# A hybrid decoder layer on one core: eight small edits of order in a kernel that keeps TensorE full

## The chip, the core and the metric

The kernel runs on one of the cores of a Trainium2 chip. Four engines compute: TensorE (PE in the profile, its weight loads PEld), VectorE (DVE), ScalarE (ACT) and GpSimd (POOL). SyncE (SP) only issues transfers. Each engine works through a queue of its own in order and waits on semaphores for the others. [...]

The metric is the time of one launch on the device in microseconds, the median of several runs. A profiled execution of the same program gives the trace, and its span runs from the first instruction to the last.

## What is computed

One decoder layer (`DEPTH` is 1) is applied to 512 prompt tokens and to 64 sample tokens (8 sequences of 8), 576 in all, with shared weights and a width of 1024. Cut to what matters:

```
u    = rms(x) * g_pre_mix
proj = u @ w_in                      # z, conv channels, dt, q, k, v, gates, og
y    = mamba2_ssd(conv(xbc), dt, state)          * silu(z), normed
h    = mlstm(q, k, v, igate, fgate, state), normed * sigmoid(og)
x    = x + rms(concat(y, h) @ w_out) * g_post_mix
x    = x + rms(cross_attention(rms(x)*g, memory) @ w_xo) * g_post_x
u    = rms(x) * g_pre_ffn
x    = x + rms((silu(u @ w_gate) * (u @ w_up)) @ w_down) * g_post_ffn
```

Everything is float32, and besides `y` the states, the convolution tails and the memory keys and values are returned.

## The kernel before

**Number format.** A float32 product is made of three: each operand is split into a high part (the rounded format that TensorE takes at full rate) and a low part, the rest. The kernel computes high·high, high·low and low·high. A weight tile of 128 x 1024 comes by DMA into a `raw` buffer (two of them, a ring), ScalarE casts the high part into a `whi` buffer (three) and VectorE, or a DMA that accumulates, makes the low part in a `wlo` buffer (three). `split_w` (lines 178 to 194) is this chain, and `gemm` (line 201) is the products: per weight block two with the high part, then one with the low part. With its argument `late` it puts the low products of the first blocks behind all of their high ones.

**Stages.** The input projection (tiles of `win`) with convolution and gates runs to about 97 us of the trace. The Mamba heads follow (`ssd_prompt`, lines 624 to 693, with the sample states beside them, lines 712 to 805), to about 252 us, while TensorE also gets the q, k, v tiles as filling work. The mLSTM heads, the z and og gates and the output projection come next, then memory keys, attention and its projection `xo` (to about 700 us), and the feed-forward part to the end. In that last part gate, up and down products are done with a scheme of seven products in place of eight (`class Seven`, from line 1803): a pair of tiles is cut into blocks, sums of blocks are split into high and low parts, and `mul` (lines 1878 to 1887) does one of the seven products, number `w` of 0 to 6. `Down` uses blocks of three weight columns (`nk` is 3); `early` does products 0, 1, 3 and 2, `late` 5 and 6, `mid` 4.

**What sets the order.** Outside of blocks under `manual_schedule` a planner orders each engine's queue: it walks through a plan in which every instruction has a cost and a priority by its place in the program, and gives an engine what is ready there. `tc.issue_after(ins)` adds an edge to this: what the block traces *on the engine of* `ins` is queued behind it. It is an order in that engine's queue, no wait for completion, and instructions on other engines get no edge. Waits on data, and on a buffer's former readers, are added by the framework. Under `manual_schedule` (from the second half of `xo` to the first pairs of the feed-forward part, and at the very end) the order is written by hand through positions given to `at_`. The planner works on the whole program, so an edit early on can move the order further down.

**Places that the edits touch.** The start (lines 303 to 341) issues products of zeros into `ps_warm`, and loads `par` (gains and small constants), two weight tiles in four pieces each and the eight pieces of `xraw`. In the gate rows (lines 524 to 582) `cumst` and `sxst` hold a row sum in three bfloat16 pieces; `sx` also goes into `r1`, whose transposes become `CT`. In `ssd_prompt` each head gets a mask `lm` of 128 x 512: four sums on VectorE (L670), an exponential on ScalarE (L672), and a product with `cbs` on VectorE (L673), kept in the list `mults`; TensorE multiplies with it in `ps_yi` (L678). Beside it GpSimd scales the sample states:

```
with tc.issue_after(mults[7].ins) if b == 2 else ExitStack():
    G.tensor_tensor(hn, hn, decs[:, :, bb:bb + 1].to_broadcast([P, 16, 64]), op=ALU.mult)
```

`z_evac` (L1050) takes a z tile out of PSUM, and its first step is a VectorE product with `rxb` (L1053). `wm_split` (L1271) loads and splits four weight tiles for the memory keys and values. `xo` (L1528) makes the projection after attention; tiles 0, 1 and 2 hold the three PSUM buffers of the pool `g`, and each is taken out by a ScalarE square (L270 or L274) and a ScalarE copy (L1540).

Of the kernel before, what the change touches and what calls it, by code (L numbers as in the profile page):

```python
# [11 lines left out]
F32 = mybir.dt.float32  # L12
F32R = mybir.dt.float32r
BF16 = mybir.dt.bfloat16
AF = mybir.ActivationFunctionType
ALU = mybir.AluOpType
# [3 lines left out]
P = 128  # L20
# [4 lines left out]
KT = 8  # L25
# [81 lines left out]

CUT = 512
CCUT = 128
NWARM = 21  # L110
NSS = 7
NWX = 3
TCOPT = dict(schedule_with_timeline_sim=True)
# [2 lines left out]
def build(nc, tc, ctx, I, O):  # L116
    V, A, G, S, TE = nc.vector, nc.scalar, nc.gpsimd, nc.sync, nc.tensor
    mm = TE.matmul
# [12 lines left out]
    def SL(slot, name, dt=F32, shape=(P, KT, T)):  # L131

        return big.tile(list(shape), dt, name=name, tag="s%d" % slot, bufs=1)
# [29 lines left out]
    def PAR(k, j=None, w=1):  # L163
        a, b = _cols[k]
        return par[:, a:b] if j is None else par[:, a + j:a + j + w]
# [12 lines left out]
    def split_w(src, n=1024, cut=CUT, acc=False, pool=None, to=None, raw=None):  # L178
        if raw is None:
            raw = wp.tile([P, 1024], F32, name="raw", tag="raw", bufs=2)  # L180
        loads.append(S.dma_start(raw[:, :n], src))
        if to:
            split(*to, raw[:, :n])
            return to
        hi, lo = hi_lo(pool)
        casts.append(A.copy(hi[:, :n], raw[:, :n]))  # L186
        for e, a, b in ((V, 0, cut), (G, cut, n)):
            if b > a and e is G and acc:

                A.activation(lo[:, a:b], hi[:, a:b].bitcast(F32), AF.Copy, scale=-1.0)  # L190
                accs.append(G.dma_start(lo[:, a:b], src[:, a:b], accum_op=ALU.add))  # L191
            elif b > a:
                e.tensor_tensor(lo[:, a:b], raw[:, a:b], hi[:, a:b].bitcast(F32), op=ALU.subtract)  # L193
        return hi, lo
# [112 lines left out]
    psw = MP("ps_warm")  # L307
    for _ in range(NWARM):
        mm(psw[:, 0:256], wz[:, 0:128], wz, start=True, stop=True, skip_group_check=True)
    S.dma_start(par, I["par"])  # L310

    wl = [wp.tile([P, 1024], F32R, name="wlo", tag="wlo", bufs=3) for _ in range(2)]
    RT = {k: wp.tile([P, 3], F32, name=k + "_r", tag=k + "_r") for k in ("px0", "p30", "px1", "p31")}
# [2 lines left out]
    for k in range(KT):  # L316
        if k % 2 == 0:
            c = slice(128 * k, 128 * k + 256)
            S.dma_start(raws[0][:, c], I["win"][1][:, c])
        xd = (S if k else A).dma_start(xraw[:, k, :], I["xT"][:, k, :])  # L320
        if k % 2 == 0:
            xd = (S if k else A).dma_start(raws[1][:, c], I["win"][2][:, c])
        if k == 0:
            with tc.issue_after(xd.ins), tc.high_priority(offset=300):

                A.activation(sp.tile([P, 1], F32, name="one"), wz[:, 0:1], AF.Exp)

        if k == 0:
            V.tensor_copy(wi[0][0][:, c], raws[0][:, c])
        for t0, n in ([(0, T)] if k else HALVES):  # L330
            ts_ = slice(t0, t0 + n)
            uhk = A.activation(uh[:, k, ts_], xraw[:, k, ts_], AF.Copy, scale=PAR("g_pre", k))
            ulk = V.scalar_tensor_tensor(ul[:, k, ts_], xraw[:, k, ts_], PAR("g_pre", k), uh[:, k, ts_].bitcast(F32),
                                         op0=ALU.mult, op1=ALU.subtract)
        if k % 2 == 0:
            for i in range(2):
                with tc.issue_after(uhk.ins), tc.issue_after(ulk.ins):
                    split(wi[i][0][:, c], wi[i][1][:, c], raws[i][:, c], cast=None if k or i else lambda *_: None)
# [219 lines left out]
    V.tensor_copy(mp[r4, 512:576].rearrange("p (c t) -> p c t", t=8), m0.unsqueeze(2).to_broadcast([4, 8, 8]))  # L558
    sx = row("sx", tag="la")
    V.tensor_tensor(sx[r4, :], cum[r4, :], mrw[r4, :], op=ALU.subtract)  # L560
    V.tensor_tensor(sx[r4, :], sx[r4, :], mp[r4, :], op=ALU.add)
    V.tensor_tensor(gpr[r4, :], ig[r4, :], cum[r4, :], op=ALU.subtract)
    V.tensor_tensor(gpr[r4, :], gpr[r4, :], mp[r4, :], op=ALU.subtract)
    r2 = row("r2", 4, tag="i2")
# [7 lines left out]
    for st_, src, n in ((cumst, cum[0:16, :], 16), (sxst, sx[r4, :], 4)):  # L572
        b0 = 32 if n == 4 else 0
        bt, d1 = btt[b0:b0 + n, :], d1t[b0:b0 + n, :]
        G.memset(st_, 0.0)
        V.tensor_copy(bt, src)
        A.copy(st_[0:n, :], bt)
        V.tensor_tensor(d1, src, bt, op=ALU.subtract)
        V.tensor_copy(bt, d1)
        A.copy(st_[32:32 + n, :], bt)  # L580
        V.tensor_tensor(d1, d1, bt, op=ALU.subtract)
        A.copy(st_[64:64 + n, :], d1)
# [41 lines left out]
    def ssd_prompt(g):  # L624
# [35 lines left out]
        for j in range(4):  # L660
            jj = g * 4 + j
            psi = MP("ps_yi")
            lms = []
            for k in range(2):
                h = 2 * jj + k
                psb = MP("ps_l")
                mm(psb, sel[:80, h:h + 1].to_broadcast([80, P]), cumst[:, 0:TP], start=True, stop=True)
                lm = sd.tile([P, 512], F32, name="lm", tag="tmp", bufs=2)
                for c in range(4):
                    V.scalar_tensor_tensor(lm[:, c * P:(c + 1) * P], psb[:, c * P:(c + 1) * P], ncum[:, c, h:h + 1],  # L670
                                           C16("maskp"), op0=ALU.add, op1=ALU.add)
                exps.append(A.activation(lm, lm, AF.Exp))  # L672
                mults.append(V.tensor_tensor(lm, lm, cbs, op=ALU.mult))  # L673
                lms.append(lm)

            for c in range(4):
                for k in (1, 0):
                    m = mm(psi[64 * k:64 * k + 64, c * P:(c + 1) * P], xdt[c][:, 2 * j + k, :], lms[k][:, c * P:(c + 1) * P],  # L678
                       start=True, stop=True, skip_group_check=True)
            inner.append(m)  # L680
            pse = MP("ps_ec")
            for k in range(2):
                mm(pse[64 * k:64 * k + 64, 0:384], sel[:80, 2 * jj + k:2 * jj + k + 1].to_broadcast([80, 64]),
                   cumst[:, P:TP], start=True, stop=True, skip_group_check=True)
            ec = sd.tile([P, 384], F32, name="ec", tag="ec", bufs=1)
            A.activation(ec, pse[:, 0:384], AF.Exp)
            psn = MP("ps_yn")
            for c in range(1, 4):
                mm(psn[:, (c - 1) * P:c * P], hs[c][:, 2 * j:2 * j + 2, :].rearrange("p h k -> p (h k)"),
                   Ct[:, c * P:(c + 1) * P], start=True, stop=True, skip_group_check=True)  # L690
            V.tensor_tensor(ec, ec, psn[:, 0:384], op=ALU.mult)
            V.scalar_tensor_tensor(y[:, jj, 0:TP], xs[:, jj, 0:TP], PAR("dskip", jj), psi, op0=ALU.mult, op1=ALU.add)
            G.tensor_tensor(y[:, jj, P:TP], y[:, jj, P:TP], ec, op=ALU.add)
# [356 lines left out]
    def z_evac(j):  # L1050
        def ev(t0, n, ps):
            t = tmp()[:, 0:n]
            V.tensor_tensor(ps, ps, rxb[:, t0:t0 + n], op=ALU.mult)  # L1053
            A.activation(t, ps, AF.Tanh, scale=0.5)
            V.scalar_tensor_tensor(t, t, 1.0, ps, op0=ALU.add, op1=ALU.mult)
            yj = y[:, j, t0:t0 + n]
            V.scalar_tensor_tensor(yj, t, 0.5, yj, op0=ALU.mult, op1=ALU.mult)
            add_sq(None, ssqg[j // 4], yj, j % 4, n, t0=t0, q=t)
        return ev
# [160 lines left out]
    turns = list(range(len(PRE)))  # L1220

    memh = at.tile([P, 2, KT, 256], F32R, name="memhl")
    memraw = SL(1, "memraw", F32, (P, KT, 256))
    rmem_b = at.tile([P, 256], F32, name="rmem_b")
    ssqm, ssq = ssq_tile("ssqm"), ssq_tile("ssqo")
    for j in range(8):
# [42 lines left out]
    wm = [(wmh[:, 16 + 1024 * i:1040 + 1024 * i], wml[:, 48 + 1024 * i:1072 + 1024 * i]) for i in range(4)]  # L1269

    def wm_split(i):  # L1271
        split_w(I["wmk"][6 + i] if i < 2 else I["wmv"][3][:, i - 2, :], to=wm[i])

    def chain2(i, js):

# [249 lines left out]
    evx = []  # L1525
    ssq = ssq_tile("ssqxo")

    def xo(j, i, pool=None):  # L1528

        t0, n = EHALVES[i]  # L1530

        with tc.issue_after(evx[j - 3].ins if j > 2 else ovs[5].ins):
            ps, w = GP("ps_xo")[:, :n], weights(("xo", j), I["wxo"][j], pool=pool, cut=1024)

        def step(k0, k1):
            m = gemm(ps, [(*w, KT)], act(oh), act(ol), t0, n, k0, k1, [2, 3, 4, 5, 6, 7, 0, 1], 6 if j == 3 else 0)
            if k1 < KT:
                return m
            add_sq(ph, ssq, ps, j if i == 0 else XO1.index(j), n, t0=t0)
            evx.append(A.activation(f[:, j, t0:t0 + n], ps, AF.Copy, scale=PAR("g_postx", j)))  # L1540
            return m, evx[-1]
        return step

    u3_ = SL(3, "u3h", F32R, (P, 5120))
# [258 lines left out]
    class Seven:  # L1803
# [74 lines left out]
        def mul(s, ps, w, b, start=True):  # L1878

            fh, fl = s.factor(w)  # L1880
            nk = s.n // P
            for k in range(nk):
                wh, wl = fh[:, k, :], fl[:, k, :]
                mm(ps, wh, b[0][k], start=start and k == 0, stop=False, skip_group_check=True)  # L1884
                mm(ps, wh, b[1][k], start=False, stop=False, skip_group_check=True)  # L1885
                m = mm(ps, wl, b[0][k], start=False, stop=k == nk - 1, skip_group_check=True)  # L1886
            return m

    class Pair(Seven):
# [503 lines left out]
```

## Time and profile before

| | |
|---|---|
| runs before | 1083.1, 1080.54, 1079.46 us, median 1080.54 |
| the profiled execution | 1079.74 us, of which the span is 1078.0 |
| granted TensorE clock, mean | 0.999 |
| TensorE | 1068.0 us busy, 99% of the span, 8124 products |
| its weight loads | 1014.8 us, 94% |
| VectorE | 752.0 us, 70% |
| ScalarE | 608.1 us, 56% |
| GpSimd | 231.0 us, 21% |
| DMA | 182.02 MB, mean 169 GB/s |

The page gives busy time by engine, then 40 slices of the span, the DMA queues, the chain of work that ended last, and the costliest groups of instructions. The timeline gives instructions in order of time: start, duration, engine, line, operation, output and inputs, shapes, count, and in brackets how long the engine stood idle before and what ended it. Consecutive instructions of one kind stand in one row with their count. The view of one line or tile gives its durations as least, median and most. A product's duration includes its way through the array, so what tells TensorE's pace is the distance from start to start.

### The profile page before, as it was taken

The numbers are of one execution on the slowest core, as the hardware profiler recorded it, in microseconds if no ns is written. First come the engines' busy times: TensorE is split into PE (matmuls) and PEld (weight loads), VectorE is DVE, ScalarE is ACT, GpSimd is POOL, SyncE is SP. The second block draws the span as 40 slices with busy tenths as digits, with TensorE's granted clock in tenths as the row PEclk, the third lists the DMA queues.
The fourth block names the chain that finished last, engine by engine and source line by source line (L and its number), as shares of the span: only waits on it lengthen the run. The fifth ranks groups of instructions, "written<-read, shape, count | busy, mean of one in ns | idle before, by whom it ended". The sixth has DMA issues, their size and how long they took to land.

```text
span 1078.0 us, 20698 instructions
## 1 busy us (share of the span) xinstructions
PE 1068.0 (99%) x8124; PEld 1014.8 (94%) x8124; DVE 752.0 (70%) x1508; ACT 608.1 (56%) x1094; POOL 231.0 (21%) x304
## 2 busy tenths in 40 slices
PE   9999999999999999999999999999999999999997
PEld 9999887778999999999999989999999999999997
DVE  6897775658877775569755546766467887787556
ACT  7867522345654555556555445645567566656653
POOL 1444643313113121000154301100011111111000
PEclk9999999999999999999999999999999999999999
DMA  6786544426654438753468775743477697578532
GB/s 208 179 168 131 157 126 175 149 71 185 190 154 144 113 113 320 233 205 105 150 202 282 277 253 179 240 131 95 135 165 155 153 203 165 118 186 186 131 132 89
DMA packets 58822, 182.02 MB, mean 169 GB/s; under 512 B 6588, under 2 KB 11836, under 8 KB 58212
## 3 DMA queue, kind: packets, MB, share of 16 engines
q1 hardware_dynamic: 42740, 138.06, 39.2%
q0 software_dynamic: 15408, 41.69, 19.9%
q8 instruction: 64, 1.05, 0.4%
q10 hardware_dynamic: 576, 0.95, 0.3%
q14 instruction: 34, 0.28, 0.1%
HBM read 160.01 MB, written 20.65 MB: 168 GB/s over the span
## 4 chain that ended last, share of the span: by engine, by line
PE 95%; DVE 2%; DMA 2%; ACT 1%; issue 0%; SPq 0%; DVEq 0%; ACTq 0%
PE ps_in L208 6%; PE ps_in L211 6%; PE ps_in L209 6%; PE ps_v L850 5%; PE ps_o L211 3%; PE ps_g L1885 3%; PE ps_u L1885 3%; PE ps_g L1884 3%; PE ps_o L209 3%; PE ps_u L1886 3%; PE ps_g L1886 3%; PE ps_o L208 3%; PE ps_u L1884 3%; PE ps_dn L1884 2%; PE ps_dn L1885 2%; PE ps_dn L208 2%
## 5 line engine op out<-in xcount | busy, mean ns | idle before, releaser
L208 PE MATMUL ps_in<-uh,whi 128*128 128x320 f32 (+1 forms) x544 | 161.6, 297 | 0.3 <-ACT la L448 0.3
L211 PE MATMUL ps_in<-uh,wlo 128*128 128x320 f32 (+1 forms) x544 | 161.6, 298 | 0.0
L209 PE MATMUL ps_in<-ul,whi 128*128 128x320 f32 (+1 forms) x544 | 161.2, 296 | 0.0
L186 ACT CAST whi<-raw 128x1024 fp32r<-128x1024 f32 (+1 forms) x104 | 105.2, 1014 | 98.8 <-PE ps_in L209 25.7
L193 DVE TENSOR_TENSOR wlo<-raw,whi 128x512 fp32r<-128x512 f32 (+1 forms) x96 | 94.1, 982 | 68.7 <-ACT whi L186 67.6
L211 PEld LDWEIGHTS ps_in<-uh,wlo 128*128 128x128 f32 x544 | 102.2, 188 | 1.7 <-issue 1.3
L208 PEld LDWEIGHTS ps_in<-uh,whi 128*128 128x128 f32 x544 | 102.3, 188 | 1.4 <-ACT la L448 0.6
L209 PEld LDWEIGHTS ps_in<-ul,whi 128*128 128x128 f32 x544 | 102.3, 188 | 1.2 <-issue 0.8
L1884 PE MATMUL ps_g<-b,whi 128*128 128x288 f32 x144 | 42.4, 295 | 0.0
L1885 PE MATMUL ps_g<-b,whi 128*128 128x288 f32 x144 | 42.4, 295 | 0.0
L1885 PE MATMUL ps_u<-b,whi 128*128 128x288 f32 x144 | 42.2, 294 | 0.0
L1884 PE MATMUL ps_u<-b,whi 128*128 128x288 f32 x144 | 42.2, 294 | 0.0
L191 POOL DMA_DIRECT2D wlo<-win x31 | 26.9, 866 | 71.1 <-ACT wlo L190 66.6
L198 DVE TENSOR_TENSOR wlo<-sw,whi 128x1024 fp32r<-128x1024 f32 (+1 forms) x26 | 29.6, 1140 | 16.7 <-ACT whi L197 16.6
L1857 ACT CAST whi<-rawx 128x1024 fp32r<-128x1024 f32 (+1 forms) x26 | 25.6, 987 | 26.5 <-PE ps_dn L1885 13.7
L208 PE MATMUL ps_xo<-qh,whi 128*128 128x288 f32 x128 | 38.3, 302 | 0.2 <-ACT whi L186 0.2
L209 PE MATMUL ps_xo<-ql,whi 128*128 128x288 f32 x128 | 37.8, 297 | 0.0
L211 PE MATMUL ps_o<-mixm_h,wlo 128*128 128x256 f32 (+1 forms) x128 | 37.7, 295 | 0.0
L209 PE MATMUL ps_o<-mixm_l,whi 128*128 128x256 f32 (+1 forms) x128 | 37.5, 293 | 0.0
L211 PE MATMUL ps_xq<-u2h,wlo 128*128 128x320 f32 (+1 forms) x128 | 37.5, 294 | 0.0
L209 PE MATMUL ps_xq<-u2l,whi 128*128 128x320 f32 (+1 forms) x128 | 37.4, 294 | 0.0
L211 PE MATMUL ps_o<-mixs_h,wlo 128*128 128x320 f32 (+1 forms) x128 | 37.4, 292 | 0.0
(769 smaller groups left out, 3841.1 us busy)
## 6 DMA issues: line engine op xcount, KB each, us to landing
raw<-win SPq DMA_DIRECT2D x35, 512.0 KB, 4.2
raw<-wout SPq DMA_DIRECT2D x17, 512.0 KB, 3.7
raw<-wxq SPq DMA_DIRECT2D x13, 512.0 KB, 4.3
raw<-wgate SPq DMA_DIRECT2D x13, 512.0 KB, 3.6
raw<-wup SPq DMA_DIRECT2D x13, 512.0 KB, 5.3
wlo<-win POOLq DMA_DIRECT2D x23, 256.0 KB, 5.3
kva<-vc SPq DMA_DIRECT2D x11, 512.0 KB, 6.1
raw<-wv SPq DMA_DIRECT2D x10, 512.0 KB, 4.0
```

The costliest lines, as they stand in the source:

```text
L186: casts.append(A.copy(hi[:, :n], raw[:, :n]))
L191: accs.append(G.dma_start(lo[:, a:b], src[:, a:b], accum_op=ALU.add))
L193: e.tensor_tensor(lo[:, a:b], raw[:, a:b], hi[:, a:b].bitcast(F32), op=ALU.subtract)
L198: (eng or V).tensor_tensor(lo, src, hi.bitcast(F32), op=ALU.subtract)
L208: mm(ps, wh, ah, start=i == 0, stop=False)
L209: mm(ps, wh, al, start=False, stop=False)
L211: m = mm(ps, tiles[order[c]][1], xh(order[c], t0, n), start=False, stop=c == len(tiles) - 1)
L850: mm(ps, a, b, skip_group_check=True, **kw)
L1857: A.copy(s.h3[:, s.all], s.r2[:, s.all])
L1884: mm(ps, wh, b[0][k], start=start and k == 0, stop=False, skip_group_check=True)
L1885: mm(ps, wh, b[1][k], start=False, stop=False, skip_group_check=True)
L1886: m = mm(ps, wl, b[0][k], start=False, stop=k == nk - 1, skip_group_check=True)
```

## The change

The diff has eight parts.

1. The number of products of zeros at the start goes from 21 to 17.
2. The load of `par` goes behind the first piece of `raws[0]` in SP's queue.
3. The first subtraction for `cumst` (and for `sxst`) is queued behind the last step of `sx` on VectorE.
4. After the eighth mask product GpSimd gets a copy of one column of that mask into a tile of its own, `lm0`.
5. For the second half of z tile 0, the VectorE product with `rxb` is queued behind the sixteenth mask product.
6. The four loads of `wm_split` go into spare columns of the slot of `memraw`, in two turns, in place of the `raw` ring, each queued behind the load before it.
7. In the first half of `xo`, the taking out of tiles 0 to 2 is kept back until tile 3 begins, and there the weights of tile 3 come first.
8. In product 1 of a block with `nk` of 3 (the `Down` blocks) the six products with the high part come first and the three with the low part after them.

```diff
-NWARM = 21
+NWARM = 17
@@
         mm(psw[:, 0:256], wz[:, 0:128], wz, start=True, stop=True, skip_group_check=True)
-    S.dma_start(par, I["par"])
@@
             S.dma_start(raws[0][:, c], I["win"][1][:, c])
+        if k == 0:
+            S.dma_start(par, I["par"])
         xd = (S if k else A).dma_start(xraw[:, k, :], I["xT"][:, k, :])
@@
-    V.tensor_tensor(sx[r4, :], sx[r4, :], mp[r4, :], op=ALU.add)
+    sx_done = V.tensor_tensor(sx[r4, :], sx[r4, :], mp[r4, :], op=ALU.add)
@@
-        V.tensor_tensor(d1, src, bt, op=ALU.subtract)
+        with tc.issue_after(sx_done.ins):
+            V.tensor_tensor(d1, src, bt, op=ALU.subtract)
@@
                 lms.append(lm)
+                if len(mults) == 8:
+                    G.tensor_copy(sd.tile([P, 1], F32, name="lm0"), lm[:, 0:1])
@@
-            V.tensor_tensor(ps, ps, rxb[:, t0:t0 + n], op=ALU.mult)
+            with tc.issue_after(mults[15].ins) if t0 and j == 0 else ExitStack():
+                V.tensor_tensor(ps, ps, rxb[:, t0:t0 + n], op=ALU.mult)
@@
-    memraw = SL(1, "memraw", F32, (P, KT, 256))
+    mem1 = SL(1, "memraw", F32, (P, 4608))
+    memraw = mem1[:, 0:2048].rearrange("p (k t) -> p k t", t=256)
+    spare = [mem1[:, a:a + 1024] for a in (2048, 3072)]
@@
     def wm_split(i):
-        split_w(I["wmk"][6 + i] if i < 2 else I["wmv"][3][:, i - 2, :], to=wm[i])
+        with tc.issue_after(loads[-1].ins):
+            loads.append(S.dma_start(spare[i % 2], I["wmk"][6 + i] if i < 2 else I["wmv"][3][:, i - 2, :]))
+        split(*wm[i], spare[i % 2])
@@
+    kept_back = []
@@ def xo(j, i, pool=None):
+        if (j, i) == (3, 0):
+            with tc.issue_after(ends[0].ins):
+                weights(("xo", j), I["wxo"][j], cut=1024)
+            while kept_back:
+                kept_back.pop(0)()
@@
-            add_sq(ph, ssq, ps, j if i == 0 else XO1.index(j), n, t0=t0)
-            evx.append(A.activation(f[:, j, t0:t0 + n], ps, AF.Copy, scale=PAR("g_postx", j)))
-            return m, evx[-1]
+            at_e = len(evx)
+            evx.append(None)
+            def out():
+                add_sq(ph, ssq, ps, j if i == 0 else XO1.index(j), n, t0=t0)
+                evx[at_e] = A.activation(f[:, j, t0:t0 + n], ps, AF.Copy, scale=PAR("g_postx", j))
+            if j < 3 and i == 0:
+                kept_back.append(out)
+            else:
+                out()
+            return m, evx[at_e]
@@ def mul(s, ps, w, b, start=True):
+            late = nk if nk == 3 and w == 1 else 1
             for k in range(nk):
-                wh, wl = fh[:, k, :], fl[:, k, :]
-                mm(ps, wh, b[0][k], start=start and k == 0, stop=False, skip_group_check=True)
-                mm(ps, wh, b[1][k], start=False, stop=False, skip_group_check=True)
-                m = mm(ps, wl, b[0][k], start=False, stop=k == nk - 1, skip_group_check=True)
+                mm(ps, fh[:, k, :], b[0][k], start=start and k == 0, stop=False, skip_group_check=True)
+                mm(ps, fh[:, k, :], b[1][k], start=False, stop=False, skip_group_check=True)
+                for c in range(nk) if k == late - 1 > 0 else [k] if late == 1 else ():
+                    m = mm(ps, fl[:, c, :], b[0][c], start=False, stop=c == nk - 1, skip_group_check=True)
```

## The prediction

> **What bounds the kernel now.** I read the page's first part, then the waits of TensorE, then the timeline around each wait, because only what shortens a gap on TensorE can move the end.
>
> ```profile
> span 1078.0 us, 20698 instructions
> ## 1 busy us (share of the span) xinstructions
> PE 1068.0 (99%) x8124; PEld 1014.8 (94%) x8124; DVE 752.0 (70%) x1508; ACT 608.1 (56%) x1094; POOL 231.0 (21%) x304
> ```
>
> TensorE is busy for 1068.0 of 1078.0 us, so 10.0 us are all that no order of the other engines' work could exceed as a gain. The change removes 4 products of zeros and no real product. The waits of TensorE (who waited, for whom, us in total, times, longest) are four in the whole run:
>
> ```profile
> PE ps_yi L678 <- DVE lm L673: 1.1, 1, 1.1
> PE ps_warm L309 <- DVE wz L306: 1.1, 1, 1.1
> PE ps_in L208 <- ACT la L448: 0.3, 1, 0.3
> PE ps_xo L208 <- ACT whi L186: 0.2, 1, 0.2
> ```
>
> They lie at 1.06, 37.64, 175.07 and 637.12 us, as the timeline rows below show. "Busy" runs to the end of a product that is already overlapped by the next, so a shorter gap shows only as a longer distance from one start to the next; I looked for these too, and two of them belong to the change (844.92 and 944.88). All sums are in the time of the profiled execution, 1079.74 us (span 1078.0), which is 0.80 us under the median of the runs shown, 1080.54; I add the 0.80 at the end.
>
> **Parts 1 and 2, the start.** Timeline of TensorE at the start (start, us, engine, line, operation; x21 is a count):
>
> ```profile
> 1.06 4.66 PE L309 MATMUL ps_warm<-wz 128*128 128x256 bf16 x21 [1.06 <-DVE wz L306]
> 5.38 0.83 PE L349 MATMUL ps_in<-uh,whi 128*128 128x256 f32 x2
> ...
> 6.42 0.28 PE L350 MATMUL ps_in<-ul,whi 128*128 128x256 f32 x1
> 6.54 0.31 PE L349 MATMUL ps_in<-uh,whi 128*128 128x320 f32 x1
> ```
>
> From 1.06 to 5.38 are 4.32 us for 21 products of zeros, 0.206 each. Seventeen would end at 1.06 + 17 x 0.206 = 4.56. The first real product also needs the first piece of `raws[0]`, and SyncE's queue gives what the moved `par` is worth:
>
> ```profile
> 0.75 0.39 SPq L310 DMA_DIRECT2D par<-par  x1
> 1.20 0.41 SPq L319 DMA_DIRECT2D raw<-win  x1
> ```
>
> The piece goes out 1.20 - 0.75 = 0.45 earlier and `par` 0.45 later; everything behind them in that queue keeps its place. So the first real product can start at about 5.38 - 0.45 = 4.93. That lead of 0.45 meets the wait at 37.64:
>
> ```profile
> 37.04 0.31 PE L444 MATMUL ps_in<-ul,whi 128*40 128x320 f32 x1
> 37.64 0.39 PE L208 MATMUL ps_in<-uh,whi 128*128 128x256 f32 x1 [0.29 <-ACT la L448]
> ```
>
> The chain that ends in `la` is made, in its early part, of transfers, ScalarE and VectorE; its piece at 10.48 is a tile on its way:
>
> ```profile
> 10.48 4.87 DMA raw<-win
> ```
>
> Neither TensorE nor the moved load stands in it, so `la` comes when it came, and TensorE, arriving 0.45 earlier, waits 0.29 + 0.45 = 0.74. I take 0. The ends are a gain of 0.45 (if the wait goes) and a loss of 0.45 (if `par`, which ScalarE reads in the same microseconds, holds up the chain by its whole delay). The value near 0 is taken because the wait is there in the trace and its releaser lies on another engine.
>
> **Part 3, the first subtraction for `cumst`.**
>
> ```profile
> 75.54 0.73 DVE L578 TENSOR_TENSOR d1t<-cum,btt 16x576 f32<-16x576 f32 x1
> ```
>
> It goes behind the last step of `sx` and takes 0.73 us with it, so `sx` and its transposes come up to 0.73 earlier and `cumst` a few VectorE instructions later. `cumst` is first read by the mask sums of the Mamba stage (L667), which come after the gate rows and the rest of the convolution, and none of the four waits lies between 37.64 and 175.07 us: that work hides it. I take 0; uncovered it would be 0.73 either way.
>
> **Part 4, GpSimd after the eighth mask product.** This is the largest gap that the change can reach. VectorE and GpSimd at 172 us, and TensorE beside them:
>
> ```profile
> 172.81 2.21 DVE L673 TENSOR_TENSOR lm<-lm,cbs 128x512 f32<-128x512 f32 x1
> ```
> ```profile
> 172.54 4.27 POOL L789 TENSOR_TENSOR h<-h,vt 128x1024 f32<-128x1024 f32 x2 [6.21 <-PE ps_hs L781]
> ```
> ```profile
> 173.58 0.40 PE L792 MATMUL ps_hu<-stb,bm 96*128 96x512 f32 x1
> 175.07 1.09 PE L678 MATMUL ps_yi<-lm,xdt 128*64 128x128 f32 x16 [1.10 <-DVE lm L673]
> ```
>
> All sixteen mask products, in the view of their line (least/median/most ns):
>
> ```profile
> L673 DVE TENSOR_TENSOR lm<-lm,cbs x16: 673/680/2207, 131.6 to 248.8; 128x512 f32<-128x512 f32 x16
> ```
>
> The eighth takes 2.21 us where the median is 0.68, and it ran while GpSimd's first scaling (half of 4.27) was under way. Without that neighbour it would end at 172.81 + 0.68 = 173.49, before TensorE issues its `ps_hu` product. A product that is not held up is followed by the next within its own duration, 0.40 at most here; by the steps of products of 512 columns I take 0.23 as an estimate (twice the 0.12 of the 256 columns above), so of 175.07 - 173.58 = 1.49 us a gap of 1.26 goes.
>
> [...]
>
> Does the copy bring that about? It reads `lm` after the product, so it waits for it on GpSimd, and what stands behind it in GpSimd's queue waits as well: the two scalings (they start about 173.6 in place of 172.54, some 1.1 late), then L693. GpSimd was idle for 6.21 us before and their readers on VectorE come last of all in this group, so the 1.1 us late costs nothing that TensorE waits for; next in line is the VectorE sum of `ps_hu` into `h`, up to 1.1 late. But nothing ties the scaling to the copy. The present `issue_after(mults[7])` names a VectorE instruction while the scaling is on GpSimd, so it orders nothing, and the copy stands there by the planner's priorities only. The scaling is released by `ps_hs`, which the planner put on TensorE ahead of five `ps_v` products; the mask product is later in its plan. So the copy may be put behind the first scaling. I take the gain of 1.26 as the likelier by a little, since the program's place of the copy is ahead of the scaling's. The ends: a gain of 1.26, and a loss of one more mask product of this kind, 2.21 - 0.68 = 1.53, if a moved scaling meets the next one.
>
> **Part 5, the z tile behind the sixteenth mask product.**
>
> ```profile
> 247.83 0.49 DVE L1053 TENSOR_TENSOR ps_in<-ps_in,rxb 128x320 f32<-128x320 f32 x1
> 248.22 1.28 DVE L673 TENSOR_TENSOR lm<-lm,cbs 128x512 f32<-128x512 f32 x2
> ```
> ```profile
> 247.94 0.63 ACT L672 ACTIVATE lm<-lm 128x512 f32<-128x512 f32 x1 [0.40 <-DVE lm L670]
> ```
> ```profile
> 249.30 0.28 PE L211 MATMUL ps_in<-uh,wlo 128*128 128x256 f32 x1
> 249.65 0.55 PE L678 MATMUL ps_yi<-lm,xdt 128*64 128x128 f32 x6
> ```
>
> The product with `rxb` takes 248.22 - 247.83 = 0.39 of VectorE's queue. Without it mask fifteen starts at 247.83, and mask sixteen when its exponential is through, 247.94 + 0.63 = 248.57 and a little, ending near 249.30. `ps_yi` could then follow its neighbour at one step, 249.41 in place of 249.65: gain 0.24. Late next is this product with `rxb` itself, by 1.4 us; a PSUM buffer waits for it, and no wait near it shows. The ends are 0 and 0.24, and a loss of 1.4 if that buffer is wanted at once.
>
> **Part 6, the loads of `wm_split`.** Four tiles leave the `raw` ring, so other tiles can be loaded earlier into it and these four wait for `memraw` to be read. No TensorE wait lies between 175 and 637 us. Behind these loads in SyncE's queue stand the loads of `x` and of the next tiles, which wait with them if `memraw` comes free late; the products of the memory keys and of the output projection hide that. I take 0. If the cover goes, a tile late by a whole transfer costs up to the 4.87 of the transfer above; a gain is excluded, since there is no gap to close.
>
> **Part 7, `xo`.**
>
> ```profile
> 635.32 0.41 ACT L270 ACTIVATE ssqxo<-ps_xo 128x288 f32<-128x288 f32 x1 [2.99 <-PE ps_xo L211]
> 635.63 0.49 ACT L1540 ACTIVATE f_xo<-ps_xo,par 128x288 f32<-128x288 f32 x1
> 636.01 1.05 ACT L186 CAST whi<-raw 128x1024 fp32r<-128x1024 f32 x1
> ```
> ```profile
> 636.57 0.29 PE L211 MATMUL ps_xo<-qh,wlo 128*128 128x288 f32 x1
> 637.12 0.40 PE L208 MATMUL ps_xo<-qh,whi 128*128 128x288 f32 x1 [0.25 <-ACT whi L186]
> ```
>
> The gap is 637.12 - 636.57 = 0.55 against a step of 0.13, so 0.42. The cast can start at 635.32 in place of 636.01 and end at 636.37. But tile 3 writes into the PSUM buffer of tile 0, which is read by the square and the copy, and these now stand behind the cast: 636.37 + 0.31 + 0.49 = 637.17. One wait takes the place of the other. I take 0; the ends are a gain of 0.42 and a loss of two further pairs of square and copy, 2 x 0.69 = 1.4.
>
> **Part 8, product 1 of a `Down` block.**
>
> ```profile
> 844.38 0.84 ACT L197 CAST whi<-sw 128x768 fp32r<-128x768 f32 x1 [0.65 <-PE ps_dn L1885]
> ```
> ```profile
> 844.92 0.29 PE L1886 MATMUL ps_dn<-te,wlo 128*128 128x288 f32 x1
> 845.27 0.40 PE L1884 MATMUL ps_dn<-hh,whi 128*128 128x288 f32 x1
> ```
> ```profile
> 944.75 0.30 PE L1885 MATMUL ps_dn<-te,whi 128*128 128x288 f32 x1
> 944.88 0.29 PE L1886 MATMUL ps_dn<-te,wlo 128*128 128x288 f32 x1
> 945.23 0.40 PE L1884 MATMUL ps_dn<-hh,whi 128*128 128x288 f32 x1
> ```
>
> The cast overwrites a high part that product 1 reads, and was released by its last such product (L1885). With the six high products first, that last one comes two places, 2 x 0.13 = 0.26, earlier: cast 844.12 to 844.96. TensorE wants the result at 844.92 + 0.13 = 845.05, so the gap of 845.27 - 845.05 = 0.22 goes, and the same at 945.23: gain 0.44. The ends are 0 (the low parts are not there, or the cast is held by something else) and 0.44; in other blocks two products fewer stand ahead of a wait for a low part, a loss of up to 0.26 each, and none of the four waits lies there.
>
> **The sum.** 0 + 0 - 1.26 - 0.24 + 0 + 0 - 0.44 = -1.94. From 1079.74 to 1077.80, and with the 0.80 to the median 1078.6.
>
> **The rivals.** *The copy lands behind the scaling.* Then the change doesn't do what it is named for: the mask product stays at 2.21 us and only 0.24 + 0.44 = 0.68 is left, 1079.9. For it: the missing edge, and the plan's order on TensorE. Against: the copy comes first in the program.
>
> *The clock.* After 4.56 TensorE is idle for some 0.37 us. Steps of 0.206 us turn into 6.54 - 6.42 = 0.12 by 6.5 us, 5.5 us after the first product. If the gap starts this anew, full pace comes at 4.93 + 5.5 = 10.4, 3.9 us at about half pace, 1.9 us of work lost; 0.74 of waiting at 37.64 takes some of it, so +1.2: 1079.8. Against it: the clock may not care for so short a gap. [...]
>
> *Slower: splits between the mask sums.* A new order on VectorE from 97 us on, since parts 3 to 5 change its plan. In that stage it also makes low parts of weights, by the groups of 97 to 252 us (us in all, mean ns):
>
> ```profile
> L193 DVE TENSOR_TENSOR wlo<-raw,whi 128x1024 fp32r<-128x1024 f32 (+1 forms) x19 | 21.2, 1125 | 8.9 <-ACT whi L186 8.9
> ```
>
> Each split that newly falls between a head's sums and its mask product holds TensorE for up to 1.13 us, for the filling products there are counted out. From two on (2.3 against 1.94) the kernel is slower than before; with five it is 1080.54 - 1.94 + 5.6 = 1084.2. Against it: sixteen heads have only one visible wait now, so there is slack at most of them.
>
> *The start's gain also carries.* If the transfers behind `la` gain too, another 0.45 + 0.29 = 0.74: 1077.9.
>
> **How the numbers follow.** All parts as worked out 0.40, the copy behind the scaling 0.28, the clock 0.06, splits 0.18, the start's gain 0.08. The forecast is the first: 1078.6. The low end is this less the further gains that I took at 0 (0.74 at the start, 0.42 in `xo`) and less some 1 us between the runs shown: 1076.4. The high end takes in the second and third case and two to three splits up to 1082.5; beyond it lie the worse half of the splits. The likeliest case's own range is 1077.4 to 1079.6. A difference under 0.3%, 3.2 us, is about what a measurement of this kernel can tell from none. Faster than 1077.3 come 0.12 of the first case by that scatter and 0.04 of the last, 0.16; slower than 1083.8 come 0.12 of the splits and 0.05 where the moved scaling (1.53) and a tile of part 6 (4.87) cost what they can, 0.17; the rest, 0.67, is within.
>
> **What would show it.** The mask product after 172 us at 0.68 and `ps_yi` with no wait (part 4); GpSimd's copy before or behind the first scaling; the wait for `la` grown to 0.7; `ps_yi` one step after its neighbour near 249; the wait at 637 naming a PSUM buffer in place of the weights; no gap at 845 and 945; steps of 0.12 by 6.5 us. The prediction is wrong if new waits for `lm` or for weights stand in TensorE's list, above all between 97 and 252 us.

## The result

The changed kernel takes 1085.01 us (median; 1084.4 to 1086.1) against 1080.55 for the kernel before, a ratio of 1.004 with a 95% interval of 1.0029 to 1.0051, so 4.3 us slower (3.1 to 5.5). Beside other kernels a second time it was 1.0036 (1.0025 to 1.0048). 1078.6 had been forecast, at most 1082.5. The first part of the page after:

```profile
span 1083.2 us, 20699 instructions
## 1 busy us (share of the span) xinstructions
PE 1069.1 (99%) x8120; PEld 1013.8 (94%) x8120; DVE 752.4 (69%) x1508; ACT 608.5 (56%) x1094; POOL 231.0 (21%) x305
```

The work is the same, four products of zeros less. What has changed is the list of TensorE's waits (who, for whom, us in total, times, longest): nine rows in place of four.

```profile
PE ps_yi L682 <- DVE lm L675: 1.1, 1, 1.1
PE ps_warm L309 <- DVE wz L306: 1.1, 1, 1.1
PE ps_dn L1909 <- DVE f_ffn L2009: 1.0, 4, 0.3
PE ps_in L350 <- ACT uh L333: 1.0, 1, 1.0
PE ps_in L208 <- ACT la L449: 0.8, 1, 0.8
PE ps_os L1444 <- DMA kva<-vc: 0.7, 1, 0.7
PE ps_dn L1909 <- ACT whi L197: 0.6, 2, 0.3
PE ps_os L1444 <- ACT kva L1469: 0.3, 1, 0.3
PE ps_ss L234 <- DVE ssqx L275: 0.2, 1, 0.2
```

The first row is the one that the change is named for, and it is still there. Pairing the products of both traces in order (the n-th real product of the one with the n-th of the other) gives where the lag grows: 0.47 us at the first real product, 1.7 by 38 us, 1.55 at 600 us, 1.2 more between 603 and 630 us (`ps_os`), 0.15 back in `xo` and behind it, and 2.7 more in two places of the feed-forward part. That makes 5.2 between these two executions, against 4.3 in the times.

**The start.** `uh` is the high part of the input, which the first real products read. `par` is read by every scaling that makes `uh` (L333 after, L332 before), since its scale `g_pre` lies in `par`. ScalarE and TensorE after:

```profile
5.29 0.96 ACT L333 ACTIVATE uh<-xraw,par 128x256 fp32r<-128x256 f32 x2 [2.12 <-DMA par<-par]
```
```profile
1.06 3.81 PE L309 MATMUL ps_warm<-wz 128*128 128x256 bf16 x17 [1.06 <-DVE wz L306]
5.85 0.87 PE L350 MATMUL ps_in<-uh,whi 128*128 128x256 f32 x2 [0.98 <-ACT uh L333]
```

The scalings started at 4.05 before and at 5.29 now, held by `par`, and TensorE stands idle for 0.98. `par` was issued 0.44 later than before, but its first reader on ScalarE starts 1.6 later (3.70 before, 5.29 now). The first `xraw` transfer, which ScalarE issues at 0.74 in both kernels, also lands later. In the chain of work (start, us, what), before and after:

```profile
0.74 3.29 DMA xraw<-xT
```
```profile
0.74 4.17 DMA xraw<-xT
...
4.92 0.33 SPq L321
...
6.72 4.99 DMA xraw<-xT
11.72 5.23 DMA raw<-win
```

SyncE's seventh transfer is released by that landing, at 4.92 in place of 4.05, and everything behind it in the queue moves with it. The two transfers that come next in the chain also take longer, 4.99 and 5.23 in place of 4.62 and 4.87. So the chain to `la`, which the prediction took as fixed, ends 1.7 later, 0.87 of it by the queue and 0.73 by these two:

```profile
38.28 0.31 PE L445 MATMUL ps_in<-ul,whi 128*40 128x320 f32 x1
39.36 0.39 PE L208 MATMUL ps_in<-uh,whi 128*128 128x256 f32 x1 [0.78 <-ACT la L449]
```

**GpSimd's copy** stands behind both scalings, and the mask product is as slow as before:

```profile
174.17 4.27 POOL L793 TENSOR_TENSOR h<-h,vt 128x1024 f32<-128x1024 f32 x2 [6.21 <-PE ps_hs L785]
178.39 0.18 POOL L678 COPY lm<-lm 128x1 f32<-128x1 f32 x1
```
```profile
174.44 2.21 DVE L675 TENSOR_TENSOR lm<-lm,cbs 128x512 f32<-128x512 f32 x1
```

**The feed-forward part.** ScalarE before, and then after, where the first block behind a set of hidden sums begins:

```profile
841.42 1.14 ACT L197 CAST te<-gt 128x1152 fp32r<-128x1152 f32 x1
842.46 0.51 ACT L197 CAST u3h<-d 128x384 fp32r<-128x384 f32 x1
```
```profile
844.13 0.51 ACT L197 CAST u3h<-d 128x384 fp32r<-128x384 f32 x1
844.55 1.15 ACT L197 CAST te<-gt 128x1152 fp32r<-128x1152 f32 x1
```

The two casts have changed places. `te` holds hidden sums of the third pair, and `u3h` takes the high part of the fourth weight block; the low part of `te` is made on VectorE behind the cast. With `te` late, four of the six products with `te` that had filled the time before the next wait are put behind that wait. TensorE after:

```profile
846.85 0.43 PE L1909 MATMUL ps_dn<-te,whi 128*128 128x288 f32 x2
847.59 0.41 PE L1909 MATMUL ps_dn<-hh,whi 128*128 128x288 f32 x1 [0.31 <-ACT whi L197]
...
848.62 0.29 PE L1912 MATMUL ps_dn<-te,wlo 128*128 128x288 f32 x1
849.20 0.40 PE L1909 MATMUL ps_dn<-hh,u3h 128*128 128x288 f32 x1 [0.28 <-DVE f_ffn L2009]
```

From 846.98 (the second product of the first row, one step of 0.13 behind) to 847.59 are 0.61, so 0.48 lost; from 848.62 to 849.20 another 0.45; a third gap of 0.43 follows at 853.41, and the three come again some 101 us later with 0.47, 0.45 and 0.34. That is 2.6; the first step behind each gap is 0.1 longer than the others, 0.6 more. The kernel before had two gaps of 0.22, each with its 0.1. So 3.2 - 0.6 = 2.6 us are lost.

### The profile page after: what moved, and what is told of

Same layout as the page of the kernel before. It is cut to its first block, busy times and chain, and to the rows that moved or that the text cites. A ratio compares the mean times of both kernels' runs of the same rounds, so it can differ in the third digit from the quotient of the medians.

```text
span 1083.2 us, 20699 instructions
## 1 busy us (share of the span) xinstructions
PE 1069.1 (99%) x8120; PEld 1013.8 (94%) x8120; DVE 752.4 (69%) x1508; ACT 608.5 (56%) x1094; POOL 231.0 (21%) x305
## 4 chain that ended last, share of the span: by engine, by line
PE 90%; DMA 4%; DVE 2%; ACT 2%; issue 1%; SPq 0%; DVEq 0%; ACTq 0%
PE ps_in L211 6%; PE ps_in L208 6%; PE ps_in L209 6%; PE ps_v L854 4%; PE ps_o L211 3%; PE ps_o L209 3%; PE ps_o L208 3%; PE ps_u L1910 3%; PE ps_u L1912 3%; PE ps_u L1909 3%; PE ps_g L1910 3%; PE ps_g L1909 3%; PE ps_g L1912 3%; PE ps_dn L208 2%; PE ps_dn L211 2%; PE ps_dn L209 2%
## 5 line engine op out<-in xcount | busy, mean ns | idle before, releaser
L186 ACT CAST whi<-raw 128x1024 fp32r<-128x1024 f32 (+1 forms) x104 | 105.1, 1013 | 99.6 <-PE ps_in L209 25.6
L1861 ACT CAST whi<-raw 128x1024 fp32r<-128x1024 f32 (+1 forms) x26 | 25.6, 983 | 21.4 <-PE ps_g L1910 10.0
```

The source lines that it names most:

```text
L1861: s.c1 = A.copy(s.h1[:, s.all], s.r1[:, s.all])
```

## The experiments

Theory S: the place of `par` costs the start its 1.7 us. Theory D: part 8 turns the casts over, and the late `te` costs its 2.6. Against both stood the rival that the losses come from arriving at another moment, and not from these edits. All ratios are to the kernel before, with 95% intervals.

**Parts 1 and 2 alone.** `NWARM = 17` and `par` behind the first piece.

> The kernel before with parts 1 and 2 alone (17 products of zeros, par behind the first tile piece). Theory S (par is late for the uh scalings, and SyncE's seventh transfer starts when the first one in its queue has landed): first real product at 5.85 instead of 5.38, the seventh SyncE transfer at 4.9 instead of 4.05, the wait for la at 0.9 instead of 0.45, and 1.7 us slower in all. The prediction's reading (la comes when it came): 0.

Measured: 1.0021 (1.0010 to 1.0032), 2.3 us. In the trace the first real product comes at 5.89, the wait for `la` loses 0.94 and the lag is 1.3: theory S, a little under its figure in the trace, over it in the times. The traced execution is the fastest of the twelve (1081.09, median 1082.30), so what the others lost beyond that does not stand in it.

**Part 8 alone.**

> The kernel before with part 8 alone. Theory D (in the first block after the hidden sums the reordered products make the planner put the cast of the fourth weight block ahead of the cast of te, so the products with te lose their place as fillers): four stalls of 0.4 to 0.5 us near 845, 847, 852 and again near 945, 947, 952, and 2.2 to 2.6 us slower. The prediction: 0.44 faster. Rival (the loss in the changed kernel came from arriving at another moment): within 0.3 of before.

Measured: 1.0026 (1.0017 to 1.0035), 2.8 us. Gaps of 0.47, 0.45, 0.41 and 0.47, 0.45, 0.45, with the casts turned over as above. The lag ahead of them is 0.0, so the loss belongs to part 8 and not to another moment of arrival.

**Part 8 in one block of each group.** The same code with one more condition, for the second block and then for the first:

```diff
-late = nk if nk == 3 and w == 1 else 1
+late = nk if nk == 3 and w == 1 and s.j == 2 else 1
```

> Part 8 in the second block of each group alone (columns 2 and 3), where the other queues keep their order. Theory D: the cast at 844.4 comes 0.26 earlier, the gaps of 0.22 at 845.0 and 945.0 are gone, 0.4 us faster and no stall elsewhere. Rival (high products first is bad in itself, by the low part's place): slower by 0.2 or more.

Measured: 0.9996 (0.9987 to 1.0006), too small for the times. The forecast of 0.4 lies within that interval. The trace has both gaps closed; at the first:

```profile
844.35 0.84 ACT L197 CAST whi<-sw 128x768 fp32r<-128x768 f32 x1 [0.38 <-PE ps_dn L1885]
```
```profile
845.15 0.29 PE L1887 MATMUL ps_dn<-te,wlo 128*128 128x288 f32 x1
845.29 0.35 PE L1884 MATMUL ps_dn<-hh,whi 128*128 128x288 f32 x1
```

0.14 from start to start where it had been 0.35. The step that the prediction worked out for the cast holds in this block.

> Part 8 in the first block of each group alone (columns 0 and 1). Theory D: here the order of the te casts turns over, and most of the loss of part 8 comes with this block: 1.2 to 2.6 us slower, with stalls on f_ffn near 848 and 852. Rival (the loss belongs to the blocks behind): within 0.3 of before.

Measured: 1.0031 (1.0019 to 1.0043), 3.3 us, with the casts turned over and gaps of 0.52, 0.87, 0.53 and 1.14. All of part 8's loss, within the intervals, comes with the first block.

**Part 8 with `te` held in its place.** The casts for the fourth weight block are queued behind that of `te` (`s.hid.cast` is the cast that `Hidden.sums` has made last):

```diff
+with tc.issue_after(s.hid.cast.ins) if isinstance(s, Down) and s.j == 0 else ExitStack():
     split(s.h4, K3(s.l3[:, s.LB]), K3(s.d4[:, 0:s.n]))
```

> Part 8 in all blocks, with the casts for the fourth weight block of the first block in each group queued behind the cast of te, so that te keeps its place ahead of them. If the late te is the cause (theory D): the waits on f_ffn and whi in the feed-forward part are gone or down to a quarter, within 0.5 of before in place of 2.8 slower. Rival (the place of the low products in the first block costs by itself, through the PSUM buffer or wacc): 1.5 or more of the 2.8 stays.

Measured: 0.9998 (0.9989 to 1.0007). The list of waits has no row for `ps_dn`, and the only gaps in the feed-forward part are the old two of 0.22. So the order of the casts is the cause; the low products' place costs nothing. It gains nothing either in this version: four products with `te` lie ahead of the wait, where the prediction counted six (847.41 to 847.80, the others went ahead), and the two gaps that part 8 was to close stand.

**Part 1 alone, and part 2 alone.**

> The kernel before with part 1 alone (17 products of zeros, par still first). Theory S (the place of par costs the 1.35 to 1.7 us of the start, the number of products of zeros nothing): first real product at 5.4 as before, with TensorE idle before it, SyncE's seventh transfer at 4.05, within 0.3 us of before. Rival clock (the idle gap starts the run-in to full pace anew): first real product at 5.4, steps of 0.12 us only from about 10 us on, 1 us or more slower.

Measured: 0.9996 (0.9986 to 1.0006). First real product at 5.31, TensorE idle for 0.44 ahead of it.

> The kernel before with part 2 alone (par behind the first tile piece, 21 products of zeros). Theory S: the scalings uh start at 5.3 instead of 4.05, the first real product at 5.85, SyncE's seventh transfer at 4.9, the wait for la near 0.9, 1.3 to 1.7 us slower, all that the start lost. Rival clock: within 0.3 of before, since the products of zeros reach up to the first real product again.

Measured: 1.0005 (0.9996 to 1.0014), although its trace has the late `uh`, the seventh transfer at 4.76 and a lag of 1.3. Each alone costs little in the times, both together 2.3: they don't add up, and theory S is not the whole of it. So the two were run again side by side.

> Parts 1 and 2 alone, again beside part 2 alone. If the place of par is the whole loss: this and the other are equal within 0.1%, both 1 to 1.5 us slower than before. If fewer products of zeros add to it (2.3 us before against 0.5 of part 2 alone): this one 1 to 2 us slower than the other, and steps on TensorE slower than 0.12 us behind its idle microsecond.

> Part 2 alone, beside parts 1 and 2. If the place of par is the whole loss: 1 to 1.5 us slower than before, as the other. If fewer products of zeros add to it: 0 to 0.5.

Measured: both edits 1.0019 (1.0009 to 1.0028), part 2 alone 1.0001 (0.9993 to 1.0010). The 1.3 to 1.7 us that theory S gave to part 2 alone reach the end of its first interval (1.5) and lie outside the second (1.1). In its second trace the scalings start at 4.83, the seventh transfer at 4.31, and the lag at 38 us is -0.2: the late `par` does not cost its 1.3 in every execution. The trace of both edits shows what had not been seen in the first:

```profile
1.06 3.81 PE L309 MATMUL ps_warm<-wz 128*128 128x256 bf16 x17 [1.06 <-DVE wz L306]
5.61 1.09 PE L350 MATMUL ps_in<-uh,whi 128*128 128x256 f32 x2 [0.74 <-ACT uh L333]
6.50 0.41 PE L351 MATMUL ps_in<-ul,whi 128*128 128x256 f32 x1
6.71 0.41 PE L350 MATMUL ps_in<-uh,whi 128*128 128x256 f32 x1
```

The steps of the 256-column products stay at 0.21 until 10.07 us, and only then fall to 0.12: six products are at work in each microsecond from 7 to 10 us, where part 2 alone has nine or ten, and 17 from 10 to 12, where it has 18. Part 2 alone, with 21 products of zeros:

```profile
1.06 3.85 PE L309 MATMUL ps_warm<-wz 128*128 128x256 bf16 x21 [1.06 <-DVE wz L306]
5.39 0.87 PE L350 MATMUL ps_in<-uh,whi 128*128 128x256 f32 x2 [0.48 <-ACT uh L333]
6.09 0.28 PE L351 MATMUL ps_in<-ul,whi 128*128 128x256 f32 x1
```

Here full pace came within the products of zeros (21 in 3.85 us, in place of 4.66 in the kernel before), and 0.48 of idle time did not end it. With both edits the lag grows from 0.6 at the sixth real product to 1.9 at 10.07, so about 1.3 is lost in products at half pace. Of the five traces with both edits this one shows it; the other four have steps of 0.14 and 0.12 by 7.1 us, after idle times of 0.98 to 1.48. The times of its single executions lie in 1080.2 to 1081.6 and 1082.7 to 1084.5, but those of the kernel before beside it also run from 1079.4 to 1083.2, and the traced execution (1084.29) lost 2.1 more between 420 and 545 us. How often the late pace falls in an execution without a trace can't be read from this, so its share in the 2 us stays open; that the 2 us need both edits is what the times show.

What sets the late pace apart is not shown. The length of the idle time alone does not, since it is longer in the other four traces. With part 1 alone, behind 0.44 us of it, the steps are 0.21 up to 6.57 us and 0.15 at most from 6.77 on. All this is read from single traces; no run sets the pace.

**Parts 3 to 7 alone.** The changed kernel without parts 1, 2 and 8.

> The changed kernel without parts 1, 2 and 8 (parts 3 to 7 alone). If parts 6 and 7 cause the stalls at 604.6, 627.5 and 628.8 of the changed kernel (ps_os waiting for vc and kva, 1.1 us together): they stand here too and the kernel is 0.7 to 1.1 slower than before. If they came from when the transfers happened to run in that execution or from the shift of 1.7 us: no wait for vc here, and -0.2 (part 5: 0.24, part 7: up to 0.12). The mask product at 172.8 stays at 2.2 us in both cases, since GpSimd's copy stands behind both scalings.

Measured: 0.9992 (0.9983 to 1.0001), 0.9 us, of which the trace of the whole change explains 0.3 (parts 5 and 7, below); the interval includes 0. No wait for `vc`, and the mask product at 2.2 us.

**The changed kernel again, without part 8, and without parts 1 and 2.**

> The changed kernel once more, for a second trace. If the stalls of ps_os near 605, 627 and 629 belong to the change (with its lag of 1.7 us at that place), they stand here again and the lag grows by about 1.1 there. If they were that execution's transfers: none of them here, and the profiled execution is about 1 us shorter for it. Start and feed-forward part lose the same in both cases (1.3 to 1.7, and 2.4).

Measured: 1.0036 (1.0025 to 1.0048). No stall of `ps_os`; the lag is 1.0 at the start, 1.0 more with a wait of the output projection for `f_mix` near 425 us, and 2.8 more in the feed-forward part. The 1.2 us at 603 to 630 of the first trace belong to that execution. Such losses of 0.5 to 1.2 us, near 425 and 455 us too, stand in some traces and not in others, also of kernels that differ from before nowhere near: the trace of part 8 with `te` held has a wait of `ps_os` for `kva` of 0.6.

> The changed kernel without part 8. Theory D: the stalls of 0.4 to 0.5 near 847, 849, 853 and 948, 950, 955 are gone, and the two of 0.22 near 846 and 946 are back: 2.4 us faster than the changed kernel, 1.5 to 2.2 slower than before. Rival (the loss in the feed-forward part comes from the shift of the start): the stalls stay.

Measured: 1.0004 (0.9994 to 1.0013), 0.4 us, less than the 1.5 to 2.2 expected; about 2.1 for the start and -0.9 for parts 3 to 7 make 1.2, which lies within the interval. The gaps in the feed-forward part are the old two of 0.22.

> The changed kernel without parts 1 and 2. Theory S: first real product at 5.3, la waits 0.25 to 0.9 as in the kernels with par first, 1.3 to 1.7 faster than the changed kernel, so 2.2 to 2.9 slower than before. If the stalls of ps_os at 605 to 629 come with the shift of the start: none here. If with parts 6 and 7: they stand.

Measured: 1.0014 (1.0005 to 1.0023), 1.5 us, less than the 2.2 to 2.9 expected; 2.8 for part 8 and -0.9 for parts 3 to 7 make 1.9, which lies within.

**The scalings tied to the copy.** The kernel before with part 4, and the edge put on GpSimd:

```diff
-with tc.issue_after(mults[7].ins) if b == 2 else ExitStack():
+with tc.issue_after(lm0[0].ins) if b == 2 else ExitStack():
     G.tensor_tensor(hn, hn, decs[:, :, bb:bb + 1]...
```

> The kernel before with part 4, and the two scalings queued behind the copy (an edge on GpSimd, where the name of the change says that they wait). The prediction's step: the mask product takes 0.68 instead of 2.21, ps_yi follows at 173.8 with no wait, 1.26 faster. Rival (the scalings, 1.1 later, hold up the sums behind them or meet another mask product): the mask product at 0.68, and a new gap on TensorE of up to 1.5 behind it, 0 in all.

Measured: 0.9989 (0.9980 to 0.9998), 1.2 us faster. GpSimd, VectorE and TensorE:

```profile
175.88 0.19 POOL L676 COPY lm<-lm 128x1 f32<-128x1 f32 x1 [7.24 <-DVE lm L673]
176.06 3.83 POOL L791 TENSOR_TENSOR h<-h,vt 128x1024 f32<-128x1024 f32 x2
```
```profile
175.13 0.68 DVE L673 TENSOR_TENSOR lm<-lm,cbs 128x512 f32<-128x512 f32 x1
```
```profile
175.90 0.40 PE L794 MATMUL ps_hu<-stb,bm 96*128 96x512 f32 x1
176.22 1.09 PE L680 MATMUL ps_yi<-lm,xdt 128*64 128x128 f32 x16
```

With the scaling behind it the mask product is back at 0.68, and `ps_yi` follows after 0.32 in place of 1.49. That is the step of the prediction, with 1.17 for its 1.26, once the order is really there.

**What gained, together.** Copy with the edge, part 5, part 7, and the high products first in the second blocks.

> The kernel before with what the earlier runs showed to gain: the two scalings queued behind the copy (1.26), part 5 (0.24), part 7 (0.12 of its gap of 0.41), and the high products first in the second block of each group alone (0.44). Sum 2.06 faster, if the gains add up; if the work behind takes them back, between 0.5 and 1.5.

Measured: 0.9981 (0.9970 to 0.9992), 2.1 us faster than the kernel before (0.9 to 3.2), as the sum said. The list of waits has lost `ps_yi` and `ps_xo`; the last two rows are of the kind that comes and goes with the execution:

```profile
PE ps_warm L309 <- DVE wz L306: 1.1, 1, 1.1
PE ps_in L208 <- ACT la L448: 0.7, 1, 0.7
PE ps_o L211 <- DVE wlo L193: 0.7, 1, 0.7
PE ps_ss L234 <- DVE ssqm L275: 0.4, 1, 0.4
```

## The prediction, point by point

- **Parts 1 and 2 (taken as 0, measured about 2): wrong.** The step that failed is "the first real product also needs the first piece of `raws[0]`": it needs `uh` too, and `uh` needs `par`, so the scalings started 1.2 later in that trace. The loss of 0.45 at most fell with it, since with the larger piece ahead the first `xraw` also landed later and, through it, SyncE's queue moved. The sentence that neither TensorE nor the moved load stands in the chain to `la` is wrong for the load. But this step alone does not make the 2 us: part 2 alone measured 1.0005 and 1.0001. They come only with part 1 too, which was taken as free, and how they divide between the late `uh` and the late pace stays open. The rival on the clock, put at 0.06, had full pace at 10.4, and one trace has it at 10.07; its 1.9 us of work lost were about 1.3. Its condition, that an idle time starts the run-in anew, does not hold: four traces that were idle for longer have full pace by 7.1 us.
- **Part 3 (0): right as far as the traces go.** The lag is 1.7 at 82 us and 1.7 again at 88; the bump between them comes of products that have changed places, not of lost time.
- **Part 4 (-1.26, at little better than even): wrong, and the rival "the copy lands behind the scaling" is right.** It lands behind both. The price was right, as the tied version shows. What makes the mask product slow beside the scaling is not shown; in the trace before, the two that begin while GpSimd scales `h` (at 144.03 and 172.81) take 1.64 and 2.21 us, the other fourteen 0.67 to 0.69.
- **Part 5 (-0.24): right in kind.** The distance to `ps_yi` went from 0.35 to 0.20, so 0.15 was gained where 0.24 was forecast:

```profile
251.00 0.28 PE L211 MATMUL ps_in<-uh,wlo 128*128 128x256 f32 x1
251.20 1.09 PE L682 MATMUL ps_yi<-lm,xdt 128*64 128x128 f32 x16
```

- **Part 6 (0): no loss shown.** The waits near it in single traces stand in kernels without part 6 as well.
- **Part 7 (0): nearly.** One wait took the place of the other, as worked out, but it is 0.13 shorter, 0.42 in place of 0.55 from start to start; the weight load now waits for the copy out of PSUM, the memory that the products are written to:

```profile
639.31 0.29 PE L211 MATMUL ps_xo<-qh,wlo 128*128 128x288 f32 x1
639.73 0.40 PE L208 MATMUL ps_xo<-qh,whi 128*128 128x288 f32 x1
```
```profile
PEld ps_xo L208 <- ACT f_xo L1560: 0.4, 1, 0.4
```

- **Part 8 (-0.44, measured +2.8): wrong.** The cast's earlier release was right: with the edit in the second blocks alone the two gaps of 0.22 are gone. What failed is the point at which TensorE wants the result: it was kept at 845.05, with six products of `te` ahead of it. The planner's new order put the cast of `te` behind that of `u3h`, and only two of the six were left there. The rival on a new order placed it on VectorE between the mask sums; it came on ScalarE, 600 us further on, at the very edit.
- **The range** reached 1082.5 and left out the case that edits taken at 0 or better lose 2 us or more: about 2 for parts 1 and 2, 2.8 for part 8, and -0.9 for the rest make the 4 that were measured.

## What to carry to other kernels

Before a load is moved back, look up every reader of its tile in the first microseconds, not only the consumer that the profile names as waiting. An edit of the order on one engine, in a program that a planner orders, is priced only once the order of the other engines' queues is known: the gain of 0.22 in each of two places was real, and a pair of casts that changed places cost six times as much. An instruction that is to hold back another needs an edge to it; its place in the program is none.

## What had not been expected of the hardware

The time at which TensorE comes to full pace varies with the execution, of kernels whose first product starts at 1.06: the steps of 0.21 us end within the products of zeros in one (part 2 alone, 21 of them in 3.85 us in place of 4.66), at 6.42 us in the kernel before and at about 6.7 with part 1 alone. With the products of zeros ending at 4.87 and 0.74 us idle behind them full pace came at 10.07 in one execution, and by 7.1 us in four others that were idle for longer. With the order of the first transfers in SyncE's queue goes the landing of one that ScalarE issues at 0.73 or 0.74 us in either case: SyncE's seventh transfer, which waits for it, starts at 4.01 to 4.39 in ten traces with `par` first and at 4.31 to 5.28 in seven with the larger piece first. And the product behind a gap is followed after 0.23 us where the others are after 0.13 (845.27 in the kernel before, 847.59 after). With the first gap closed, by part 8 in the second blocks, the step there is still 0.19, so not all of the 0.1 is the gap's.
